# Where a feed-forward product begins in PSUM, and when its turned operand is read back

## The chip, the cores and the metric

One core of one Trainium2 chip runs the whole program. The metric is the device time of one execution in microseconds (us), from launch to end. The profile is one further execution of the same program, recorded by the hardware profiler; its span is counted from the first to the last instruction, and times of single instructions are given from the span's start.

## The reference, cut to what matters

Two transformer layers are computed for 256 tokens of width 2048, in fp32. Each layer has a mixer (sparse and linear attention in the first, stick-breaking attention in the second), then a gated feed-forward part, then a gated projection of a side input. The change lies in the feed-forward part alone, which is run once in each layer with hidden width 5632:

```
def _swiglu(h, norm_g, w_gate, w_up, w_down):
    xn = _rmsnorm(h, norm_g)
    return (jax.nn.silu(xn @ w_gate) * (xn @ w_up)) @ w_down
```

## The kernel before

**Products.** Every fp32 operand is split into a high part and a low rest, and a product is the sum of three matmuls (high by high, high by low, low by high; L235 to L237). Weights arrive in tiles `raw` of 1 MB by SyncE's queue, in three buffers that take turns. ScalarE casts half a tile at a time to `whi` (L106), VectorE subtracts to get `wlo` (L107), and TensorE runs 12 matmuls of 512 columns on the pair. Such a half tile of work is called a half unit here. There are four buffers of `whi` and of `wlo`, so that ScalarE and VectorE run some half units ahead of TensorE.

**Blocks of the feed-forward part** (`ffn`). The 11 column blocks of 512 hidden units stand in groups of three, three, three and two. `gate_up` computes one hidden block: both 128-token halves of gate and of up. The first block is computed plainly (`gate_up_8`); the ten others use a scheme with seven in place of eight products on a part of the rows (`gate_up_7`), with sums of weights that VectorE makes in the tile `work` (L858 to L860), and matmuls at L849. `down` multiplies the hidden blocks of one group by 512 columns of the third weight and adds the result to `h` (L268). While the hidden blocks of one group are computed, the four `down` blocks of the group before are put between them: one after the first hidden block, one after the second, two after the third; the group of two gets two after each. So there are eight places in a layer where a `down` block follows a `gate_up_7` directly, four of them followed by one `down` block and four by two (in layer 0, the last `down` blocks of the program part follow behind the eighth place). The last four `down` blocks come at the end.

**PSUM.** There are eight banks of 128 x 512. `mm_tile` hands out banks 0 to 3 in turn by the counter `turns["mm"]`, and a block takes two. `gate_up_7` does not ask for banks: it writes all eight by number, the gate halves in banks 0 and 1, the up halves in banks 2 and 3. When the gate is complete, VectorE adds a correction to banks 0 and 1, and when the up product is complete, to banks 2 and 3 (both L902, two banks at once). The first matmul into a bank waits until its last reader is done. Since the counter is not touched by `gate_up_7`, the bank with which the next `down` begins depends on how many blocks were handed out before.

**The way of the hidden block.** After the second L902, VectorE multiplies by the silu of the gate (L930, tile `sl`). The block has to be turned, tokens against hidden units, for `down`. `cross` does it with 32 x 32 transposes on VectorE into `tq` (L143), four transfers to DRAM (`ty`, L147) and two back (`tx`, L151), all six issued by GpSimd. `split_hid` then reads `tx` back: ScalarE casts it to `hH` (L920), VectorE subtracts to `hL` (L921).

**What sets the order.** `later` puts a step into a list, and `tick`, called after each half unit, runs the head of the list when it is due; `need` runs it at once. `split_hid` is due so many half units after `cross` ran. This is the order in which the program is written; a scheduler then sets each engine's own order, from what it takes to be ready when. Each engine works through its own list in that order.

Of the kernel before, what the change touches and what calls it, by code (L numbers as in the profile page):

```python
# [27 lines left out]
def trunk_kernel(ctx: ExitStack, tc: tile.TileContext, x, p, even_norm, even_w_in, even_w_gk,  # L28
# [16 lines left out]
    turns = {"mm": 0, "at": 0}  # L45
# [74 lines left out]
    def rstd_of(key):  # L120
        if key not in rstds:
            v = sm.tile([P, NT], F32, name="var")
            nc.vector.tensor_reduce(v, ss[key], axis=AX.X, op=OP.add)
            nc.vector.tensor_scalar(v, v, 1.0 / D, EPS, op0=OP.mult, op1=OP.add)
            r = sm.tile([P, NT], F32, name="rstd")
            nc.gpsimd.tensor_tensor(r, v, mhalf[:, :NT], OP.pow)
            rstds[key] = r
        return rstds[key]
# [56 lines left out]
    def later(fn, key=None, delay=2, after=None):  # L185

        fill.append((key, state["unit"] + delay, after, fn))

    def need(key):
        while key not in done:  # L190
            run_fill()
# [17 lines left out]
    def unit(ps, stat, k0, cols, first, last, nk=KU, kw0=None, step=KU, pre=None, begun=0):  # L209


        kw0 = k0 if kw0 is None else kw0
        raw = raw_tile()
        n = sum(w for _, _, w in cols)
        for j in range(0, nk, step):
            o = 0
            for wt, c0, w in cols:
                nc.sync.dma_start(raw[:, j:min(j + step, nk), o:o + w],
                                  wt[(kw0 + j) * P:(kw0 + min(j + step, nk)) * P, c0:c0 + w]
                                  .rearrange("(k q) n -> q k n", q=P))  # L220
                o += w
        for j in range(0, nk, 2):
            hi = wp.tile([P, 2, NB], F32R, name="whi")
            lo = wp.tile([P, 2, NB], F32R, name="wlo")
            split_sb(raw[:, j:j + 2, :n], hi[:, :, :n], lo[:, :, :n])
            if pre:
                pre(k0 + j + 2)
            for c in range(2):
                k = k0 + j + c
                for tt in range(NT):  # L230
                    sh = stat[0][:, k, tt * P:(tt + 1) * P]
                    sl = stat[1][:, k, tt * P:(tt + 1) * P]
                    st = first and tt >= begun and j + c == 0
                    en = last and j + c == nk - 1
                    nc.tensor.matmul(ps[tt][:, :n], sh, hi[:, c, :n], start=st, stop=False)  # L235
                    nc.tensor.matmul(ps[tt][:, :n], sh, lo[:, c, :n], start=False, stop=False)  # L236
                    nc.tensor.matmul(ps[tt][:, :n], sl, hi[:, c, :n], start=False, stop=en)  # L237
            tick()
# [588 lines left out]
    def ffn(i, xs, nkey, nx_fn, fp):  # L827
        nblk = FF // NB
        groups = [list(range(a, min(a + 3, nblk))) for a in range(0, nblk, 3)]
        hT = {}  # L830
# [20 lines left out]
        def pair(j, b):  # L851

            raw = raw_tile().rearrange("p (r c) n -> p r c n", r=2)
            for c, w in enumerate((ffn_w_gate[i], ffn_w_up[i])):
                nc.sync.dma_start(raw[:, :, c], w[2 * j * P:(2 * j + 2) * P, b * NB:(b + 1) * NB]
                                  .rearrange("(k q) n -> q k n", q=P))

            nc.vector.tensor_tensor(T[:, 0:2], raw[:, 0], raw[:, :, 1], OP.add)  # L858
            nc.vector.tensor_tensor(T[:, 2], T[:, 1], raw[:, 0, 0], OP.add)
            nc.vector.tensor_tensor(T[:, 3], T[:, 2], raw[:, 1, 0], OP.add)  # L860

            def tok(c, t):
                return [x[:, 2 * j + c, t * P:(t + 1) * P] for x in xs]

            def comb(n):
                return [ST[:, hl, n, j] for hl in range(2)]

            pieces = [(raw[:, 0, 0:1], [(B1, tok(0, 0))]), (T[:, 0:2], [(B5, comb(0)), (B7, comb(2))]),
                      (T[:, 2:4], [(B6, comb(1)), (B4, tok(1, 1))]),
                      (raw[:, 1], [(B2, tok(1, 0)), (B3, comb(3))])]  # L870
            for n, (src, ps) in enumerate(pieces):
                hi = wp.tile([P, 2, NB], F32R, name="whi")
                lo = wp.tile([P, 2, NB], F32R, name="wlo")
                split_sb(src, hi[:, :len(ps)], lo[:, :len(ps)])
                for c, (p, stat) in enumerate(ps):
                    product(p, stat, hi[:, c], lo[:, c], j == 0, j == NS - 1 and p >= B1)
                if n % 2:
                    tick()

        def gate_up_7(b):  # L880
            need(("sT", i))
            rest = [(n, k) for n in range(2) for k in range(2 * NS, KC, KU)]

            def classical(n, k):
                nk = min(KU, KC - k)
                unit([bank[:, 2 * n], bank[:, 2 * n + 1]], xs, k, [((ffn_w_gate[i], ffn_w_up[i])[n], b * NB, NB)],
                     n == 1 and k == 2 * NS, k + nk == KC, nk=nk, begun=1)

            for j in range(NS):
                pair(j, b)  # L890
                if j < NS - 1:
                    classical(*rest.pop(0))
            nc.scalar.copy(E[:, 0], bank[:, B1])
            nc.vector.tensor_tensor(E[:, 2], bank[:, B6], E[:, 0], OP.add)
            nc.vector.tensor_tensor(E[:, 1], bank[:, B7], E[:, 2], OP.add)
            nc.vector.tensor_tensor(E[:, 3], bank[:, B5], E[:, 1], OP.subtract)
            nc.vector.tensor_tensor(E[:, 2], bank[:, B5], E[:, 2], OP.subtract)
            for n in range(2):
                while rest and rest[0][0] == n:
                    classical(*rest.pop(0))  # L900
                e = E[:, 2 * n:2 * n + 2]
                nc.vector.tensor_tensor(e, bank[:, 2 * n:2 * n + 2], e, OP.add)  # L902
                if n == 0:
                    sl = fp.tile([P, NT, NB], F32, name="sl", bufs=1)
                    for tt in range(NT):
                        nc.scalar.activation(sl[:, tt], E[:, tt], AF.Silu, scale=rstd_of(nkey)[:, tt:tt + 1])
            return sl, [E[:, 2 + tt] for tt in range(NT)]

        def gate_up_8(b):
            pg = block(xs, [(ffn_w_gate[i], b * NB, NB)], key=nkey)  # L910
            rs = rstd_of(nkey)
            sl = fp.tile([P, NT, NB], F32, name="sl", bufs=1)
            for tt in range(NT):
                nc.scalar.activation(sl[:, tt], pg[tt], AF.Silu, scale=rs[:, tt:tt + 1])
            later(sums_of_operand, key=("sT", i))
            return sl, block(xs, [(ffn_w_up[i], b * NB, NB)])

        def split_hid(dst, x, k0):
            d = [dst[n][:, k0:k0 + 4, :].rearrange("p m (q r) -> p m q r", q=8) for n in range(2)]
            nc.scalar.copy(d[0], x)  # L920
            nc.vector.tensor_tensor(d[1], x, d[0].bitcast(F32), OP.subtract)  # L921

        def gate_up(gi, n):
            b = groups[gi][n]
            if n == 0:
                hT[gi] = (fp.tile([P, 12, NT * P], F32R, name="hH"), fp.tile([P, 12, NT * P], F32R, name="hL"))
            sl, pu = gate_up_7(b) if b else gate_up_8(b)
            rs = rstd_of(nkey)
            for tt in range(NT):
                nc.vector.scalar_tensor_tensor(sl[:, tt], pu[tt], rs[:, tt:tt + 1], sl[:, tt], op0=OP.mult,  # L930
                                               op1=OP.mult)
            x = {}
            later(lambda: x.update(x=cross(sl, fp)), key=("xT", i, b))
            later(lambda: split_hid(hT[gi], x["x"], 4 * n), key=("hT", i, b), after=(("xT", i, b), 10))

        def down(gi, cb, nx):
            for b in groups[gi]:
# [8 lines left out]
        for gi, g in enumerate(groups):  # L946
            for n in range(len(g)):
                gate_up(gi, n)
                if gi:
                    for cb in range(4 * n // len(g), 4 * (n + 1) // len(g)):  # L950
                        down(gi - 1, cb, None)
# [162 lines left out]
```

## Time and profile before

| | |
|---|---|
| median of 3 runs | 2458.12 us (2457.89 to 2463.89) |
| profiled execution, its own time | 2457.39 us |
| span of the profiled execution | 2455.7 us |
| TensorE matmul busy | 2394.8 us, 98% of the span |
| VectorE busy | 1718.6 us, 70% |
| ScalarE busy | 1259.2 us, 51% |
| mean granted TensorE clock | 0.995 of full speed |

Busy time is the sum of an engine's instructions. The feed-forward part of layer 0 lies at about 390 to 1120 us of the span, that of layer 1 at about 1610 to 2345 us. A line "PE bank L235 <- DVE work L902" says that TensorE's matmul of line 235, writing a bank, waited for VectorE's instruction of line 902.

### The profile page before, as it was taken

The page shows a single profiled execution, that of the slowest core. Times are in us where ns is not written, and L with a number is a line of the kernel's source. Part 1 is how long each engine was busy: PE and PEld are TensorE (multiplying, and loading weights), DVE is VectorE, ACT ScalarE, POOL GpSimd, SP SyncE. Part 2 cuts the span into 40 slices and gives each one's busy share as a digit, 9 for nine tenths or more (in the row PEclk, how much of TensorE's full clock was granted, in tenths as well). Part 3 has the DMA queues.
Part 4 walks back from the last instruction along what each step waited for, and adds up shares of the span by engine and source line. Part 5 has one row for each costly group of instructions (what it writes and reads, how often), then busy time and mean ns, then how long its engine had stood idle before and what let it go on. Part 6 is the DMA issues. An engine that isn't in the chain of part 4 may idle for free.

```text
span 2455.7 us, 28118 instructions
## 1 busy us (share of the span) xinstructions
PE 2394.8 (98%) x10786; PEld 1965.8 (80%) x10786; DVE 1718.6 (70%) x2009; ACT 1259.2 (51%) x1560; POOL 105.3 (4%) x177
## 2 busy tenths in 40 slices
PE   8999999999999999999999999999899999999998
PEld 7887788777888888888888888887688888878887
DVE  4765556878877877755666666568778788777565
ACT  6644444545545545446545565545444455444464
POOL 0000000000000000000000000001000000000000
PEclk9999999999999999999999999999999999999999
DMA  6454465566666666555554545656566666666563
GB/s 210 149 164 154 147 213 189 182 204 206 207 230 206 206 223 222 192 194 180 173 188 162 170 165 172 206 171 209 178 208 218 216 206 214 214 223 204 180 233 121
DMA packets 240681, 473.13 MB, mean 193 GB/s; under 512 B 12849, under 2 KB 19729, under 8 KB 240418
## 3 DMA queue, kind: packets, MB, share of 16 engines
q1 hardware_dynamic: 232514, 447.07, 54.7%
q0 software_dynamic: 7744, 23.08, 2.9%
q8 instruction: 84, 1.38, 0.2%
q10 hardware_dynamic: 288, 1.18, 0.1%
q14 instruction: 51, 0.42, 0.1%
HBM read 457.66 MB, written 13.63 MB: 192 GB/s over the span
## 4 chain that ended last, share of the span: by engine, by line
PE 80%; DVE 8%; DMA 7%; ACT 3%; issue 2%; POOL 0%; SPq 0%; DVEq 0%; POOLq 0%; ACTq 0%
PE bank L235 23%; PE bank L236 23%; PE bank L237 23%; PE bank L849 8%; DVE wlo L107 3%; DMA raw<-in_ffn_w_up_dram 3%; DMA tx<-ty 1%; DMA raw<-in_odd_w_in_dram 1%; DMA ty<-tq 1%; DVE work L902 1%; PE bank L165 1%; DVE kT L135 1%; ACT whi L106 1%; DVE sl L930 1%; DVE tq L143 0%
## 5 line engine op out<-in xcount | busy, mean ns | idle before, releaser
L107 DVE TENSOR_TENSOR wlo<-raw,whi 128x1024 fp32r<-128x1024 f32 (+2 forms) x848 | 982.3, 1172 | 481.6 <-ACT whi L106 477.6
L106 ACT CAST whi<-raw 128x1024 fp32r<-128x1024 f32 (+2 forms) x848 | 843.1, 1011 | 852.7 <-PE bank L237 583.7
L235 PE MATMUL bank<-whi,aH 128*128 128x512 f32 (+2 forms) x2176 | 850.2, 391 | 1.1 <-ACT whi L106 1.1
L236 PE MATMUL bank<-wlo,aH 128*128 128x512 f32 (+2 forms) x2176 | 843.1, 388 | 4.8 <-DVE wlo L107 4.5
L237 PE MATMUL bank<-whi,aL 128*128 128x512 f32 (+2 forms) x2176 | 842.2, 387 | 0.0
L236 PEld LDWEIGHTS bank<-wlo,aH 128*128 128x128 f32 x2176 | 409.7, 188 | 89.0 <-DVE wlo L107 8.8
L235 PEld LDWEIGHTS bank<-whi,aH 128*128 128x128 f32 x2176 | 409.6, 188 | 85.3 <-issue 2.8
L237 PEld LDWEIGHTS bank<-whi,aL 128*128 128x128 f32 x2176 | 409.1, 188 | 84.6 <-issue 1.0
L235 PE MATMUL bank<-whi,hH 128*128 128x512 f32 x704 | 276.6, 393 | 16.9 <-DVE work L902 16.9
L236 PE MATMUL bank<-wlo,hH 128*128 128x512 f32 x704 | 276.2, 392 | 0.0
L237 PE MATMUL bank<-whi,hL 128*128 128x512 f32 x704 | 276.1, 392 | 0.0
L106 ACT CAST whi<-work 128x1024 fp32r<-128x1024 f32 x120 | 126.4, 1053 | 188.8 <-PE bank L237 126.3
L107 DVE TENSOR_TENSOR wlo<-work,whi 128x1024 fp32r<-128x1024 f32 x120 | 146.6, 1221 | 65.8 <-ACT whi L106 65.4
L849 PE MATMUL bank<-whi,sT 128*128 128x512 f32 x480 | 171.1, 396 | 11.7 <-ACT whi L106 11.7
L235 PEld LDWEIGHTS bank<-whi,hH 128*128 128x128 f32 x704 | 132.2, 188 | 50.3 <-ACT whi L106 19.8
L236 PEld LDWEIGHTS bank<-wlo,hH 128*128 128x128 f32 x704 | 132.3, 188 | 28.4
L237 PEld LDWEIGHTS bank<-whi,hL 128*128 128x128 f32 x704 | 132.3, 188 | 28.0
L849 PEld LDWEIGHTS bank<-whi,sT 128*128 128x128 f32 x480 | 91.6, 191 | 32.4 <-ACT whi L106 13.4
L849 PE MATMUL bank<-wlo,sT 128*128 128x512 f32 x240 | 95.1, 396 | 3.2 <-DVE wlo L107 3.2
L858 DVE TENSOR_TENSOR work<-raw 128x1024 f32<-128x1024 f32 x60 | 73.3, 1222 | 34.6 <-DMA raw<-in_ffn_w_up_dram 34.2
L147 POOL DMA_DIRECT2D ty<-tq x88 | 48.5, 561 | 1140.8 <-DVE tq L143 988.7
L849 PE MATMUL bank<-wlo,aH 128*128 128x512 f32 x180 | 72.7, 404 | 7.0 <-DVE wlo L107 7.0
(253 smaller groups left out, 1624.7 us busy)
## 6 DMA issues: line engine op xcount, KB each, us to landing
raw<-in_ffn_w_down_dram SPq DMA_DIRECT2D x88, 1024.0 KB, 5.7
raw<-in_ffn_w_gate_dram SPq DMA_DIRECT2D x48, 1024.0 KB, 5.2
raw<-in_ffn_w_up_dram SPq DMA_DIRECT2D x48, 1024.0 KB, 5.2
raw<-in_odd_w_in_dram SPq DMA_DIRECT2D x48, 1024.0 KB, 5.1
raw<-in_ffn_w_gate_dram SPq DMA_DIRECT2D x80, 512.0 KB, 3.9
raw<-in_ffn_w_up_dram SPq DMA_DIRECT2D x80, 512.0 KB, 5.3
raw<-in_even_w_in_dram SPq DMA_DIRECT2D x36, 1024.0 KB, 5.0
raw<-in_ple_w_gate_dram SPq DMA_DIRECT2D x28, 1024.0 KB, 5.1
```

What stands on the lines that cost most here:

```text
L106: nc.scalar.copy(hi, raw)
L107: nc.vector.tensor_tensor(lo, raw, hi.bitcast(F32), OP.subtract)
L135: nc.vector.transpose(dst[32 * a:32 * a + 32, :, :, 32 * q:32 * q + 32], src.rearrange("p t (m a c) -> p t m a c", a=4, c=32)[32 * q:32 * ...
L147: nc.gpsimd.dma_start(y[:, :, q].rearrange("a c t n -> c a (t n)"), tq[32 * q:32 * q + 32].rearrange("c a t m r -> c a (t m r)"))
L165: nc.tensor.transpose(ps[:, c, tt, :], h[:, tt, k * P:(k + 1) * P], ident)
L235: nc.tensor.matmul(ps[tt][:, :n], sh, hi[:, c, :n], start=st, stop=False)
L236: nc.tensor.matmul(ps[tt][:, :n], sh, lo[:, c, :n], start=False, stop=False)
L237: nc.tensor.matmul(ps[tt][:, :n], sl, hi[:, c, :n], start=False, stop=en)
L849: nc.tensor.matmul(bank[:, p], a, b, start=first and m == 0, stop=last and m == 2)
L858: nc.vector.tensor_tensor(T[:, 0:2], raw[:, 0], raw[:, :, 1], OP.add)
L902: nc.vector.tensor_tensor(e, bank[:, 2 * n:2 * n + 2], e, OP.add)
L930: nc.vector.scalar_tensor_tensor(sl[:, tt], pu[tt], rs[:, tt:tt + 1], sl[:, tt], op0=OP.mult, op1=OP.mult)
```

## The change

Two lines. At the end of `gate_up_7` the counter of banks is set to 0, so that the block behind it begins with banks 0 and 1. And `split_hid` becomes due 16 half units after its `cross` ran, not 10.

```diff
--- before.py
+++ after.py
@@ -904,6 +904,7 @@
                     sl = fp.tile([P, NT, NB], F32, name="sl", bufs=1)
                     for tt in range(NT):
                         nc.scalar.activation(sl[:, tt], E[:, tt], AF.Silu, scale=rstd_of(nkey)[:, tt:tt + 1])
+            turns["mm"] = 0
             return sl, [E[:, 2 + tt] for tt in range(NT)]
 
         def gate_up_8(b):
@@ -931,7 +932,7 @@
                                                op1=OP.mult)
             x = {}
             later(lambda: x.update(x=cross(sl, fp)), key=("xT", i, b))
-            later(lambda: split_hid(hT[gi], x["x"], 4 * n), key=("hT", i, b), after=(("xT", i, b), 10))
+            later(lambda: split_hid(hT[gi], x["x"], 4 * n), key=("hT", i, b), after=(("xT", i, b), 16))
 
         def down(gi, cb, nx):
             for b in groups[gi]:
```

TensorE's order at the first `down` block of layer 0, with the engines whose semaphores a row waits for; the rows above are the end of `gate_up_7`. First before, then with the change:

```order
L237 MATMUL bank<-whi,aL 128x512
L235 MATMUL bank<-whi,hH 128x512 [waits DVE_49,Activation_49,Pool_49]
L236 MATMUL bank<-wlo,hH 128x512
L237 MATMUL bank<-whi,hL 128x512
L235 MATMUL bank<-whi,hH 128x512
```

```order
L237 MATMUL bank<-whi,aL 128x512
L235 MATMUL bank<-whi,hH 128x512 [waits Activation_49,Pool_49]
L236 MATMUL bank<-wlo,hH 128x512 [waits DVE_49]
L237 MATMUL bank<-whi,hL 128x512
L235 MATMUL bank<-whi,hH 128x512
```

The first matmul of the block no longer waits for VectorE; the second one waits for it instead, for its own `wlo`. Before, 12 first matmuls of `down` blocks have the wait for VectorE (six in each layer), with the change none has. No matmul is added or removed.

VectorE's order after the hidden block that ends group 0 (third block of each layer): the transpose `tq` behind the products with the silu. First before, then with the change, where lines behind 906 are numbered one higher:

```order
L902 TENSOR_TENSOR work<-bank,work 128x1024
L107 TENSOR_TENSOR wlo<-raw_3966,whi 128x1024
L930 SCALAR_TENSOR_TENSOR sl<-work,rstd,sl 128x512 x2
L107 TENSOR_TENSOR wlo<-raw,whi 128x1024
L143 STREAM_TRANSPOSE tq<-sl 128x8x4x32
L107 TENSOR_TENSOR wlo<-raw,whi 128x1024
L859 TENSOR_TENSOR work<-work,raw 128x512
```

```order
L902 TENSOR_TENSOR work<-bank,work 128x1024
L107 TENSOR_TENSOR wlo<-raw_3964,whi 128x1024
L931 SCALAR_TENSOR_TENSOR sl<-work,rstd,sl 128x512 x2
L107 TENSOR_TENSOR wlo<-raw,whi 128x1024 x2
L143 STREAM_TRANSPOSE tq<-sl 128x8x4x32
L859 TENSOR_TENSOR work<-work,raw 128x512
```

The transpose stands one `wlo` later. The read-back of the same block, further down in VectorE's list:

```order
L107 TENSOR_TENSOR wlo<-work,whi 128x1024
L860 TENSOR_TENSOR work<-work,raw 128x512
L921 TENSOR_TENSOR hL<-tx,hH 128x1024
L107 TENSOR_TENSOR wlo<-work,whi 128x1024
L107 TENSOR_TENSOR wlo<-raw,whi 128x1024 x2
L894 TENSOR_TENSOR work<-bank,work 128x512
```

```order
L107 TENSOR_TENSOR wlo<-work,whi 128x1024
L860 TENSOR_TENSOR work<-work,raw 128x512
L107 TENSOR_TENSOR wlo<-work,whi 128x1024
L922 TENSOR_TENSOR hL<-tx,hH 128x1024
L107 TENSOR_TENSOR wlo<-raw,whi 128x1024
L894 TENSOR_TENSOR work<-bank,work 128x512
```

The read-back `hL` stands one `wlo` later, and in ScalarE's list `hH` stands one `whi` later at the same place. The read-back of the block before it (second block of each layer) stands where it stood. Of the 22 read-backs of the program, 12 keep their place and 10 move by one cast on ScalarE and by one to two rows on VectorE.

## Rows read from the trace of the kernel before

**Rows 1.** The page: span and instructions.

```profile
span 2455.7 us, 28118 instructions
```

**Rows 2.** Waits, whole span, TensorE's and ScalarE's: us in total, times, longest.

```profile
PE bank L235 <- DVE work L902: 16.9, 12, 1.4
PE bank L849 <- ACT whi L106: 11.7, 4, 3.7
PE bank L849 <- DVE wlo L107: 10.2, 12, 2.5
...
ACT hH L920 <- DMA tx<-ty: 24.5, 5, 6.7
```

**Rows 3.** Timeline of TensorE: start, us, line, tiles, idle before and its releaser.

```profile
575.18 0.47 PE L235 MATMUL bank<-whi,hH 128*128 128x512 f32 x1 [1.41 <-DVE work L902]
...
591.75 0.40 PE L849 MATMUL bank<-whi,aH 128*128 128x512 f32 x1
...
633.02 0.39 PE L237 MATMUL bank<-whi,aL 128*128 128x512 f32 x1
633.25 0.39 PE L235 MATMUL bank<-whi,hH 128*128 128x512 f32 x1
```

**Rows 4.** The chain of work that ended last: start, us, what; L902 pieces.

```profile
573.81 1.24 DVE work L902
...
633.45 1.23 DVE work L902
...
692.28 1.24 DVE work L902
...
768.40 1.23 DVE work L902
...
828.02 1.23 DVE work L902
...
886.82 1.24 DVE work L902
...
1858.03 1.22 DVE work L902
...
1917.59 1.23 DVE work L902
...
2053.31 1.23 DVE work L902
...
2112.15 1.24 DVE work L902
```

**Rows 5.** Timeline of VectorE behind the hidden block that ends at 573.6 us.

```profile
573.81 1.23 DVE L902 TENSOR_TENSOR work<-bank,work 128x1024 f32<-128x1024 f32 x1 [0.41 <-PE bank L237]
...
579.71 1.18 DVE L107 TENSOR_TENSOR wlo<-raw,whi 128x1024 fp32r<-128x1024 f32 x1
```

**Rows 6.** Timeline of TensorE, pair at 664 us.

```profile
664.29 0.50 PE L849 MATMUL bank<-wlo,aH 128*128 128x512 f32 x1 [0.22 <-DVE wlo L107]
```

**Rows 7.** Timeline of ScalarE at layer 1's second read-back.

```profile
1774.15 1.04 ACT L920 CAST hH<-tx 128x1024 fp32r<-128x1024 f32 x1 [6.34 <-DMA tx<-ty]
1775.10 1.04 ACT L106 CAST whi<-work 128x1024 fp32r<-128x1024 f32 x1
```

**Rows 8.** Timeline of TensorE at the second read-backs, layer 0 and layer 1.

```profile
553.22 0.50 PE L849 MATMUL bank<-whi,sT 128*128 128x512 f32 x1 [1.65 <-ACT whi L106]
554.67 0.50 PE L849 MATMUL bank<-wlo,sT 128*128 128x512 f32 x1 [0.95 <-DVE wlo L107]
...
1776.19 0.50 PE L849 MATMUL bank<-whi,sT 128*128 128x512 f32 x1 [3.34 <-ACT whi L106]
1777.64 0.50 PE L849 MATMUL bank<-wlo,sT 128*128 128x512 f32 x1 [0.95 <-DVE wlo L107]
```

**Rows 9.** Windows: stretch, us, busy (x) of PE, PEld, DVE, ACT, POOL, granted clock, DMA.

```profile
1778.00:1781.00 3.00, 3.00 (x9) 2.31 (x8) 3.00 (x4) 2.50 (x3) 0.00 (x0) 0.52 0.30 63
552.00:554.00 2.00, 0.50 (x1) 0.19 (x1) 1.75 (x2) 2.00 (x3) 0.00 (x0) 1.00 0.00 0
```

## The prediction, made before the changed kernel ran

> **What bounds the kernel now.** I read the page first: the span is 2455.7 us [rows 1], and TensorE's matmuls are busy for 98% of it, so only what TensorE waits for can be won. The waits come next, grouped over the whole span [rows 2]. The largest item of TensorE is the one that the first line of the change speaks of: 12 times a matmul waits for VectorE's L902, 16.9 us in all, 1.41 us each time. Behind it come 11.7 and 10.2 us of waits at L849 for `whi` and `wlo`. ScalarE's list holds the reason for part of these: its read-back cast `hH` waits 24.5 us in five instances for `tx` to land, and what stands behind it in its queue waits as well.
>
> The timeline shows the wait for L902 in place [rows 3]. At 575.18 us the first matmul of a `down` block starts after 1.41 us of idle time, since the counter gave it bank 2, which L902 is reading [rows 5]. At 633.25 us another `down` block starts 0.23 us after the last matmul of its `gate_up_7`, with no gap: there the counter stood at bank 0, and L902 reads banks 2 and 3. So the kernel already contains what the change wants everywhere: of the eight places of a layer the counter is right at two and wrong at six. The chain of work tells what this is worth. It passes through an L902 at each of the eight places. At the six it goes on to the waiting matmul; at the two (633.45 and 828.02 in layer 0 [rows 4]) TensorE does not wait for it, and the chain goes on through VectorE and a load of weights and comes back to TensorE only later.
>
> **First line: the bank.** Nothing is computed differently; 12 first matmuls lose a wait. The lists of instructions show just this: the wait for VectorE moves from the block's first matmul to its second, which waits for its own `wlo`. What takes the place of the wait? Three things could.
>
> The first is `wlo`. VectorE does L902, one `wlo`, the two products with silu, a sum and the transpose in one run, and the next `wlo` ends at 579.71 + 1.18 = 580.89 us [rows 5]. With four buffers this is the fifth half unit of the block. A block of six half units takes 591.75 - 575.18 = 16.57 us [rows 3], 2.76 each, so the fifth starts at 575.18 + 4 x 2.76 = 586.2 us now and at 584.8 without the wait. That leaves 3.9 us to spare. The Trainium skill (PSUM — Partial Sum Buffer, section "Engine vs sequencer instructions") says that the queues of ScalarE, VectorE and GpSimd are strictly first in, first out, while matmuls start in order. By that rule alone a wait that TensorE loses at L902 could come back at the next operand behind L902, and the gain would be 0 in place of 1.41; the row with 3.9 us to spare speaks against it here.
>
> The second is the bank itself. Banks 0 and 1 were last read by the first L902 of the same hidden block, before the whole up product, so they are free. After one `down` block, though, the next `gate_up_7` writes bank 1 with its thirteenth matmul, about 12 x 0.23 = 2.8 us behind the end of `down`, and VectorE must have added bank 1 to `h` by then. The cycles without a wait have this layout today, so their length includes it.
>
> The third is the loads of weights, and here there are twins to read. A cycle is the time from one L902 to the next, with one `down` and one `gate_up_7` between. With the wait it takes 633.45 - 573.81 = 59.64 us, or 828.02 - 768.40 = 59.62 [rows 4]. Without it, the four such cycles of the program take 58.83, 58.80, 59.56 and 58.84 us (692.28 - 633.45, 886.82 - 828.02, 1917.59 - 1858.03, 2112.15 - 2053.31), 59.01 in the mean. So of 1.41 us a place with one `down` keeps 59.63 - 59.01 = 0.62, between 0.07 and 0.84. The rest is lost where the pair of L849 catches up with its operand: 0.22 us show as a wait at 664.29 us [rows 6]. There are four such places in the program: 4 x 0.62 = 2.5 us, bounds 4 x 0.07 = 0.3 and 4 x 1.41 = 5.6.
>
> The other eight places have two or more `down` blocks behind them and no twin without the wait. In a second `down` VectorE has 16.57 us more in which to catch up, and the chain there goes from L902 through TensorE to the next L902, so I take the full wait: 8 x 1.41 = 11.3 us. The lower bound is that they lose as much as the others, 8 x 0.62 = 5.0.
>
> **Second line: the read-back.** It does much less than it says. The scheduler puts an instruction where it takes it to be ready, and of 22 read-backs 12 do not move and the others move by one or two rows. The first bad read-back of each layer, that of the second block, is among the 12, so its stall stays whole. The other is that of the third block, where `hH` waits 6.34 us in layer 1 [rows 7]. There TensorE waits 3.34 us for a `whi` that stands behind `hH`, then 0.95 for its `wlo` [rows 8]; in layer 0 it waits 1.65 and 0.95. With the change that `whi` stands ahead of `hH`, so six matmuls run before the stall; but the transpose stands one `wlo` later, which shifts the round trip by 1.18 us [rows 5]. In layer 1, `hH` would start at 1774.15 + 1.18 = 1775.33. The next cast starts 0.95 later, the first matmul on it 1.09 after that and the second another 1.45 (steps of [rows 7, 8]): 1778.82 us. Today the same matmul, at full clock, comes six matmuls behind 1777.64: 1779.02. So 0.2 us are won, in each layer: 0.4. Bounds: if the stall vanishes, 1.65 + 0.95 + 3.34 + 0.95 = 6.9 us, and 1.4 for the clock (below), 8.3; if the later round trip costs its 1.18 us twice and the clock falls in layer 0 too, a loss of 3.8.
>
> The clock is the open point here. After the idle 3.34 us in layer 1 the granted clock is 0.52 from 1778 to 1781 us, the lower of the two levels, 1.2 GHz of 2.4; in layer 0, around the idle 1.65 us, it is 1.00 [rows 9]. Three microseconds at 0.52 cost 3.00 x 0.48 = 1.4 us. The stall in layer 1 stays about as long (it starts six matmuls later and ends 1.2 us later), so I let the clock fall there as now. The Trainium skill (TensorE: Matmul & The Clock Gate, section "HAM oscillation — how this bites in real kernels") says that idle gaps throw TensorE back to its lower clock and that each costs a start at that level. By it a shorter gap in layer 1 would bring 1.4 us more, a longer one in layer 0 would cost 1.4; the rows show both sides, and the sum takes neither.
>
> **The sum** against the profiled execution: 11.3 + 2.5 + 0.4 = 14.2 us, so 2457.39 - 14.2 = 2443.2 us. The median of the runs shown is 0.73 us above the profiled time, within their own spread, so I predict 2443. About 0.3%, 7.4 us, is what a measurement of this kernel can tell from no change.
>
> **The rivals.**
>
> More comes back: the 12 waits go whole (16.9 us), and the second read-back stall shrinks to half with the clock kept (about 4): 2457.4 - 20.9 = 2436.5. For it: in the first group the transpose of the next block moves ahead of a sum, which gets its transfers out of the way of the loads. Against it: the twins.
>
> The loads take more: the places with two `down` blocks keep 0.62 us too, since the raw tiles come in the same rotation there: 12 x 0.62 = 7.4 us, 2450.0. For it: the four twins lose between 0.6 and 1.3 us of their 1.41. Against it: no wait at L849 is on the chain in the long cycles.
>
> Nothing is won: the wait comes back at the next `wlo`, 2457. It needs VectorE to be 3.9 us later than in [rows 5].
>
> The read-back loses its stalls altogether, also the first in each layer: the 24.5 us of ScalarE's wait go, and with them at most the 11.7 + 10.2 = 21.9 us of L849 waits [rows 2]: 2443.2 - 21.9 = 2421. It needs `hH` to move past the landing of `tx`; one cast is no such move.
>
> Slower: the later transpose lets `ty` and `tx` of the third block run into the next loads of weights, and TensorE idles longer at that one read-back in each layer. It decides only from a loss above 13.8 us in two places, 7 each, where the longest wait of `hH` in the program is 6.7 [rows 2]. With 8 each it would be 2457.4 - 13.8 + 16 = 2460; against it, the round trip has moved by one instruction.
>
> **How the numbers follow.** Forecast as summed: 0.62. More comes back: 0.13. The loads take more: 0.14, about half of it on either side of the 0.3% line at 2450.7. Nothing: 0.06. Stalls gone: 0.02. Slower: 0.03. Faster by over 0.3%: 0.62 + 0.13 + 0.02 + 0.08 = 0.85; same 0.06 + 0.06 = 0.12; slower 0.03. The range reaches to the two neighbours of the forecast, 2436 to 2451, and leaves out the last three cases and the tails.
>
> **What would show it.** The line "PE bank L235 <- DVE work L902" should be gone from TensorE's waits. Cycles with one `down` should take about 59.0 us, those with two about 74.7 where one now takes 768.40 - 692.28 = 76.12 [rows 4]. ScalarE's wait of `hH` for `tx` should stay above 20 us, with the first stall of each layer as now. The prediction is wrong if the L849 waits grow by more than 4 us, if a matmul of `down` waits for `wlo`, or if the granted clock falls at a place where it is 1.00 now.

## The result, and the profile after

The change takes 2436.55 us (median of four runs, 2435.57 to 2438.25) against 2461.01 us before (2457.89 to 2464.57) in the same comparison: ratio 0.9901, 95% interval 0.9889 to 0.9914. The profiled execution takes 2435.57 us, 21.8 us less than the profiled one of before. So it is faster, 6.5 us below the forecast, and inside the range by 0.6 us. As a gain it is 24.4 us by the ratio and 21.8 by the profiles, where 14.2 were forecast, and most of the surplus has one place.

The page and the waits of the changed kernel (us in total, times, longest), which answer to [rows 1, 2]:

```profile
span 2433.9 us, 28109 instructions
...
PE bank L849 <- DVE wlo L107: 12.3, 17, 3.0
PE bank L849 <- ACT whi L106: 5.5, 2, 3.1
...
ACT hH L921 <- DMA tx<-ty: 14.4, 4, 6.1
```

The wait of L235 for L902 is gone. That much was forecast. Not forecast is the second line: four waits of L849 for `whi` have become two, and `hH` has 14.4 us of waiting left of 24.5. To see where, I take the program apart by the second L902 of each hidden block, as in the prediction. VectorE's timeline of the change, from the third hidden block's L902 on (start, us, line, tiles; the last two rows are layer 1):

```profile
526.42 1.22 DVE L902 TENSOR_TENSOR work<-bank,work 128x1024 f32<-128x1024 f32 x1
...
568.40 1.22 DVE L902 TENSOR_TENSOR work<-bank,work 128x1024 f32<-128x1024 f32 x1
...
626.36 1.23 DVE L902 TENSOR_TENSOR work<-bank,work 128x1024 f32<-128x1024 f32 x1 [0.20 <-PE bank L237]
...
685.38 1.23 DVE L902 TENSOR_TENSOR work<-bank,work 128x1024 f32<-128x1024 f32 x1 [0.41 <-PE bank L237]
...
759.86 1.22 DVE L902 TENSOR_TENSOR work<-bank,work 128x1024 f32<-128x1024 f32 x1
...
1741.66 1.22 DVE L902 TENSOR_TENSOR work<-bank,work 128x1024 f32<-128x1024 f32 x1
...
1783.24 1.22 DVE L902 TENSOR_TENSOR work<-bank,work 128x1024 f32<-128x1024 f32 x1 [0.41 <-PE bank L237]
```

The same view of before for the third block, where [rows 4] begin one block later (the last two rows are layer 1's third and fourth block):

```profile
529.40 1.22 DVE L902 TENSOR_TENSOR work<-bank,work 128x1024 f32<-128x1024 f32 x1
...
1750.70 1.22 DVE L902 TENSOR_TENSOR work<-bank,work 128x1024 f32<-128x1024 f32 x1
...
1798.39 1.23 DVE L902 TENSOR_TENSOR work<-bank,work 128x1024 f32<-128x1024 f32 x1 [0.41 <-PE bank L237]
```

The cycle with two `down` blocks, 685.38 to 759.86, takes 74.48 us, where it took 76.12. The one before it, with one `down`, takes 59.02; the prediction said 74.7 and 59.0. But from the third block's L902 to the fourth's (called the third block's stretch below), with no `down` in between and hence no wait for L902 in either kernel, it is 568.40 - 526.42 = 41.98 us against 573.81 - 529.40 = 44.41, and in layer 1 41.58 against 47.69. These two stretches alone bring 8.5 us. All of the span's 21.8 us, from such differences: cycles with two `down` blocks 8.6 (six, 1.44 each), with one 0.6 (eight), the third block's read-back 8.5, the second block's 0.7, the stretch ahead of the first L902 2.2 (the change touches nothing there, and over the kernels below this start lies between 478.1 and 481.3 us), between the layers -0.4, and the end 1.6. The 2.2 and the -0.4 hold a matter of the clock: behind the first pair of layer 0 it is 0.57 for four microseconds before and 1.00 with the change, behind that of layer 1 it is the other way round, and 4 x 0.43 = 1.7 us each is what that is worth.

Not all of the 14.4 us is left over. At the last hidden block of layer 0 the wait of `hH` is new:

```profile
1049.56 1.05 ACT L921 CAST hH<-tx 128x1024 fp32r<-128x1024 f32 x1 [2.56 <-DMA tx<-ty]
```

There the next load of weights goes out 1.2 us behind the start of `ty`'s issue, where it went out 2.9 us behind, and the way through DRAM takes 8.0 us, where it took 5.1. TensorE does not wait there. The first line alone does the same and the second alone does not, so it is the counter that moved this load.

What happened at the third block is seen on four engines. The change, timelines of VectorE, SyncE, GpSimd and ScalarE (start, us, line, tiles, idle before), then windows of the same place in both layers (granted clock third from the end):

```profile
530.01 2.35 DVE L107 TENSOR_TENSOR wlo<-raw,whi 128x1024 fp32r<-128x1024 f32 x2
...
532.39 0.37 SPq L855 DMA_DIRECT2D raw<-in_ffn_w_gate_dram  x1
532.81 0.46 SPq L855 DMA_DIRECT2D raw<-in_ffn_w_up_dram  x1
...
533.81 2.20 POOL L147 DMA_DIRECT2D ty<-tq  x4 [39.20 <-DVE tq L143]
...
539.75 1.50 POOL L151 DMA_DIRECT2D tx<-ty  x2 [3.73 <-ACT whi L106]
...
546.50 1.04 ACT L921 CAST hH<-tx 128x1024 fp32r<-128x1024 f32 x1
...
547.00:550.00 3.00, 3.00 (x15) 2.31 (x13) 3.00 (x3) 3.00 (x5) 0.00 (x0) 1.00 0.05 18
...
1761.00:1765.00 4.00, 4.00 (x19) 3.34 (x18) 3.13 (x3) 4.00 (x5) 0.00 (x0) 1.00 0.21 78
```

Before, VectorE, GpSimd, SyncE and ScalarE:

```profile
535.29 1.18 DVE L107 TENSOR_TENSOR wlo<-raw,whi 128x1024 fp32r<-128x1024 f32 x1
...
535.66 2.19 POOL L147 DMA_DIRECT2D ty<-tq  x4 [38.97 <-DVE tq L143]
...
536.50 0.37 SPq L855 DMA_DIRECT2D raw<-in_ffn_w_gate_dram  x1
536.92 0.49 SPq L855 DMA_DIRECT2D raw<-in_ffn_w_up_dram  x1
...
543.93 1.50 POOL L151 DMA_DIRECT2D tx<-ty  x2 [6.07 <-ACT whi L106]
...
551.17 1.05 ACT L920 CAST hH<-tx 128x1024 fp32r<-128x1024 f32 x1 [4.65 <-DMA tx<-ty]
```

`hH` no longer waits, TensorE has no gap and the clock stays at 1.00, where before it fell to 0.52 in layer 1 [rows 9]. (The read-backs that [rows 7, 8] call second ones are this third block's.) The way through DRAM, from the issue of `ty` to the issue of `tx`, takes 539.75 - 533.81 = 5.94 us; before it took 543.93 - 535.66 = 8.27. What differs around it is a load of weights: 1 MB in two halves by SyncE's queue. Before, it goes out 0.8 and 1.3 us behind the issue of `ty`; now 1.4 and 1.0 us ahead of it. The `wlo` past which the transpose was moved is the last reader of a `raw` tile, and when it ends, SyncE may load into that tile: before, it ends at 535.29 + 1.18 = 536.47 us and the load goes out at 536.50; now the two `wlo` end at 530.01 + 2.35 = 532.36, and it goes out at 532.39. With the `wlo` ahead of the transpose, the load passes the `ty` transfers.

### The profile page after: what moved, and what is told of

It is laid out like the page before. It is cut to its first block, busy times and chain, and to the rows that moved or that the text cites. A ratio compares the mean times of both kernels' runs of the same rounds, so it can differ in the third digit from the quotient of the medians.

```text
span 2433.9 us, 28109 instructions
## 1 busy us (share of the span) xinstructions
PE 2393.8 (98%) x10786; PEld 1965.1 (81%) x10786; DVE 1716.8 (71%) x2009; ACT 1258.4 (52%) x1560; POOL 105.6 (4%) x177
## 3 DMA queue, kind: packets, MB, share of 16 engines
q10 hardware_dynamic: 288, 1.18, 0.1%
## 4 chain that ended last, share of the span: by engine, by line
PE 71%; DVE 11%; DMA 10%; ACT 3%; issue 3%; SPq 0%; POOL 0%; DVEq 0%; POOLq 0%; ACTq 0%
PE bank L236 20%; PE bank L235 20%; PE bank L237 20%; PE bank L849 6%; DMA raw<-in_ffn_w_up_dram 6%; DVE wlo L107 6%; DMA raw<-in_odd_w_in_dram 2%; ACT whi L106 1%; DVE kT L135 1%; PE bank L165 1%; DVE work L858 1%; DMA raw<-in_ffn_w_down_dram 1%; DMA tx<-ty 1%; DVE sl L931 1%; DVE work L902 1%
## 5 line engine op out<-in xcount | busy, mean ns | idle before, releaser
L235 PE MATMUL bank<-whi,aH 128*128 128x512 f32 (+2 forms) x2176 | 849.7, 391 | 0.7 <-ACT whi L106 0.7
L235 PEld LDWEIGHTS bank<-whi,aH 128*128 128x128 f32 x2176 | 409.8, 188 | 84.9 <-issue 2.8
L235 PE MATMUL bank<-whi,hH 128*128 128x512 f32 x704 | 277.2, 394 | 0.0
L849 PE MATMUL bank<-whi,sT 128*128 128x512 f32 x480 | 170.2, 394 | 5.5 <-ACT whi L106 5.5
L235 PEld LDWEIGHTS bank<-whi,hH 128*128 128x128 f32 x704 | 132.2, 188 | 30.0
L849 PEld LDWEIGHTS bank<-whi,sT 128*128 128x128 f32 x480 | 91.2, 190 | 25.3 <-ACT whi L106 6.3
L849 PE MATMUL bank<-wlo,sT 128*128 128x512 f32 x240 | 94.8, 395 | 1.9 <-DVE wlo L107 1.9
L849 PE MATMUL bank<-wlo,aH 128*128 128x512 f32 x180 | 73.3, 407 | 10.8 <-DVE wlo L107 10.4
```

Source lines behind the costliest of these rows:

```text
L849: nc.tensor.matmul(bank[:, p], a, b, start=first and m == 0, stop=last and m == 2)
```

## The experiments

All runs are compared with before on their own chip, and their ratios are to it. Edits are shown against the changed kernel, cut at "...". The theory of the first experiments: the order of that load and of `ty` makes the surplus. Its rival: the read-back, which also stands one cast later, makes it.

**One line of the change at a time.** The first line alone (due again after 10 half units), and the second line alone (no `turns["mm"] = 0`):

```diff
-            later(lambda: split_hid(hT[gi], x["x"], 4 * n), key=("hT", i, b), after=(("xT", i, b), 16))
+            later(lambda: split_hid(hT[gi], x["x"], 4 * n), key=("hT", i, b), after=(("xT", i, b), 10))
```

> The first line of the change alone (the counter set to 0, the read-back due after 10 half units as before). If the two lines simply add, this kernel has lost the 12 waits for L902 but has the stall at the third block's read-back in both layers as before (TensorE waits there near 1.65 and 3.3 us plus 0.95 each). By the cycles of the changed kernel that stall cost 2.4 us in layer 0 and 6.1 in layer 1, so this kernel should be 8.5 us slower than the changed one: about 2445 us, some 13 us faster than before. By the step of the prediction that gave the second line only 0.4 us it should stand at the changed kernel's time, 2436 to 2437 us.

Measured: 2448.94 us, ratio 0.9952 (0.9936 to 0.9969), 11.8 us below before by the ratio. `hH` waits as before at the third block, 5.96 us in layer 0 and 5.62 in layer 1; `ty` to `tx` takes 8.4 and 8.3 us.

```diff
-            turns["mm"] = 0
```

> The kernel before with the second line of the change alone; the counter of banks stays as it was, so the 12 waits for L902 are there (about 16.9 us of idle time on TensorE, 12 instances). Transfers theory (the late transpose puts the next 1 MB load ahead of the ty transfers): the third block's transpose stands one wlo later here too, so its read-back waits for nothing, its cycle is 41.5 to 42.5 us as in the change, and the time is 7 to 10 us below before. Additive rival by the first theory of the prediction (the read-back brings 0.4 us): within 2 us of before. If the shorter wait for L902 is needed for the effect (the load's place against ty depends on it), hH still waits above 2 us at the third block and the gain is below 5 us.

Measured: 2451.28 us, ratio 0.9962 (0.9950 to 0.9975), 9.4 us below before. The waits for L902 are there (17.3 us, 12), and the third block's stretch takes 41.97 and 42.83 us, where the whole change has 41.98 and 41.58. The two lines add up within their intervals: 11.8 + 9.4 = 21.2, with 24.4 for both. The second line is worth about as much as the first, where the prediction gave it 0.4.

**Transpose or read-back.** The second line moves two things at the third block. Four combinations with the first line in place: the run with the first line alone has neither. This one makes the transpose of the third block due 4 half units after the products with silu, not 2, and the read-back goes along behind it:

```diff
+            later(lambda: x.update(x=cross(sl, fp)), key=("xT", i, b), delay=4 if b == 2 else 2)
...
+            later(lambda: split_hid(hT[gi], x["x"], 4 * n), key=("hT", i, b), after=(("xT", i, b), 10))
```

> The first line, the read-back due after 10 half units, and the third block's turning made due two half units later. The orders of the engines at the third block are then those of the changed kernel (transpose one wlo later, read-back one cast later), and only read-backs of later blocks stand one row elsewhere. Both theories of the read-back expect the stall at the third block to be gone and 2436 us, within 2 us of the changed kernel. If something else in the 16 half units matters, it is slower by up to 8 us.

Measured: 2435.95 us, ratio 0.9904 (0.9880 to 0.9928), the time of the change; no wait of `hH` there, `ty` to `tx` 5.95 and 5.79 us. Now the read-back late and the transpose where it stood (its casts queued behind a certain `whi` and `wlo`):

```diff
...
+            later(lambda: split_hid(hT[gi], x["x"], 4 * n, mark[3, 2, 2] if b == 2 else None), key=("hT", i, b),
+                  after=(("xT", i, b), 10))
```

> As the kernel before in this call (the third block's turning two half units later in the changed kernel's order), but with the third block's transpose put back ahead of the wlo, and the read-back held where it is. Theory 1 (what counts is that this wlo frees its raw tile and so sends the next 1 MB of weights off ahead of the transfers ty, not among them): the weights are issued about 1 us behind ty again, tx lands some 2 us later, the stall is back, less the 1.4 us of matmuls that now run ahead of it: 2442 to 2445 us, with hH waiting for tx 5 to 6 us in each layer at the third block. Theory 2 (what counts is that the read-back stands one cast later): no stall at the third block, 2436 us.

Measured: 2445.11 us, ratio 0.9932 (0.9909 to 0.9956); `ty` to `tx` 8.42 and 8.47 us, `hH` waits 2.36 and 1.90, less than the 5 to 6 us that the theory named. And the transpose late, the read-back put back ahead of the last cast of `work`:

```diff
...
+                if (b, j, n) == (3, 2, 2):
+                    need(("hT", i, 2))
+                    with tc.issue_after(back[0].ins):
+                        nc.scalar.copy(hi, src)
...
```

> The counterpart: the third block's transpose stays behind the wlo as in the changed kernel, and the read-back is put ahead of the last cast of work again, where it stood before. Theory 1 (the order of load and transfer): the round trip stays short, hH waits for tx less than 1 us at the third block, and the time is 2436 to 2438 us. Theory 2 (the place of the read-back): the stall is back as before, 2444 to 2446 us, with waits of TensorE near 1.65 and 3.3 us at L849 for whi.

Measured: 2438.09 us, ratio 0.9909 (0.9889 to 0.9930); `ty` to `tx` 5.67 and 7.56 us, `hH` waits 1.06 and 4.48, where the theory named less than 1. These runs are of one chip, so the medians can be set against each other: the late transpose brings 2448.94 - 2438.09 = 10.9 and 2445.11 - 2435.95 = 9.2 us, the late read-back 3.8 and 2.1, which the scatter of these runs (2437.84 to 2447.44 in the third of the four) could make by itself. The transpose it is, for the most part. That it acts through the load is not shown by that: several things move with it.

**The load alone.** The next kernel is the changed one with the instructions of every engine in the same order. Only the load at the third block gets one dependency more, on the sum behind the transpose:

```diff
...
+                if (j, b) == (2, 3):
+                    tc.add_manual_dep(ld.ins, hold[0].ins.name, mybir.DependencyInfo(
+                        mybir.DependencyClass.Sync, mybir.DependencyReason.DATA), reason="hold")
...
+            hold[:] = [nc.vector.tensor_tensor(T[:, 2], T[:, 1], raw[:, 0, 0], OP.add)]
```

> The changed kernel with one more dependency and every engine's instructions in the same order: at the third hidden block of each layer the 1 MB load that SyncE sends 1.4 and 1.0 us before the first ty transfer must wait for the sum L859 behind the transpose, and so goes out about 0.4 and 0.8 us behind ty's issue. Transfers theory: ty to tx takes 8 to 8.7 us instead of 5.7 to 5.9, hH waits 2 to 4 us at this block again, the cycle of that block takes 44 to 46 us instead of 41.5 to 42, and the time is 4 to 8 us above that of the change, 2440 to 2444. Rival (the transpose's own place counts, the load is a bystander): ty to tx stays below 6 us, hH does not wait, and the time is within 2 us of the change.

Measured: 2448.53 us, ratio 0.9945 (0.9932 to 0.9958), 12.0 us above the change by the medians, 10.8 by the ratios. That is the transfers theory, with more than the 4 to 8 us it named. Its trace, timelines of GpSimd, SyncE, ScalarE and TensorE, a window, and the landing time of the load's second half (median us from issue):

```profile
537.80 2.20 POOL L147 DMA_DIRECT2D ty<-tq  x4 [39.84 <-DVE tq L143]
...
545.86 1.50 POOL L151 DMA_DIRECT2D tx<-ty  x2 [5.86 <-DMA ty<-tq]
...
538.14 0.37 SPq L855 DMA_DIRECT2D raw<-in_ffn_w_gate_dram  x1
538.56 0.46 SPq L855 DMA_DIRECT2D raw<-in_ffn_w_up_dram  x1
...
554.94 1.04 ACT L924 CAST hH<-tx 128x1024 fp32r<-128x1024 f32 x1 [4.36 <-DMA tx<-ty]
...
556.98 0.80 PE L849 MATMUL bank<-whi,aH 128*128 128x512 f32 x1 [3.02 <-ACT whi L106]
558.43 0.80 PE L849 MATMUL bank<-wlo,aH 128*128 128x512 f32 x1 [0.65 <-DVE wlo L107]
...
557.00:560.00 3.00, 2.35 (x5) 1.55 (x6) 3.00 (x4) 3.00 (x4) 0.00 (x0) 0.50 0.20 15
560.00:563.00 3.00, 3.00 (x9) 2.33 (x8) 3.00 (x5) 0.25 (x1) 0.00 (x0) 0.50 0.92 349
...
raw<-in_ffn_w_up_dram SPq DMA_DIRECT2D x1, 512.0 KB, 5.9
```

The two halves of the load go out 0.3 and 0.8 us behind `ty`, and `tx` is issued 8.06 us after `ty` (8.78 in layer 1). `hH` waits 4.36 us, then TensorE 3.02 and 0.65, and the clock lies at 0.50 from 557 to 563 us, which costs another 6 x 0.50 = 3.0 us. Together that is 6.7 us. The third block's stretches take 48.60 and 46.65 us, 6.6 and 5.1 more than in the change, 11.7 together, so these two places hold the whole loss. A later load could also cost by itself, so in another run it waits for a `wlo` still further down:

```diff
...
+                lo_op = split_sb(src, hi[:, :len(ps)], lo[:, :len(ps)])
+                hold[:] = [lo_op] if n == 1 else hold
```

> As the run before it, but the load waits for a wlo further behind the transpose, and goes out about 2.5 to 3 us behind ty's issue. Transfers theory: it meets the round trip later, ty to tx takes 5.5 to 7 us as at the other places with a load 2 to 3.3 us behind ty, hH waits less than 1.5 us, and the time is 0 to 3 us above that of the change, below that of the run before it. Rival (a load that is sent later costs time because its own weights land later): this run loses more than the run before it, 6 us or more above the change.

Measured: 2435.89 us, ratio 0.9897 (0.9882 to 0.9913), the time of the change, and 12.6 us below the run before it on the same chip. The same rows of this run:

```profile
534.62 2.20 POOL L147 DMA_DIRECT2D ty<-tq  x4 [37.66 <-DVE tq L143]
...
539.96 1.50 POOL L151 DMA_DIRECT2D tx<-ty  x2 [3.15 <-ACT whi L106]
...
537.26 0.37 SPq L855 DMA_DIRECT2D raw<-in_ffn_w_gate_dram  x1
537.68 0.50 SPq L855 DMA_DIRECT2D raw<-in_ffn_w_up_dram  x1
...
546.99 1.04 ACT L925 CAST hH<-tx 128x1024 fp32r<-128x1024 f32 x1
...
raw<-in_ffn_w_up_dram SPq DMA_DIRECT2D x1, 512.0 KB, 5.5
```

2.3 us later still, the load costs nothing: `ty` to `tx` takes 5.34 us, `hH` does not wait. (The scheduler also moved some of VectorE's `wlo` and sums behind the transpose by a few rows here; in the run before it no row of any engine moved.) So at this block the load costs time when it goes out 0.3 or 0.8 us into the 2.20 us in which GpSimd issues the four `ty` transfers; 1.4 us ahead of their start or 2.6 us behind it, it does not. With this the cause of the surplus is shown: it is the order of one load and four transfers. Why the transfers take longer in one order than in the other is not shown.

**The same at the second block.** The stall of the second block, 5.35 and 6.13 us of waiting of `hH`, is the same collision, if the theory holds. Its rows in the change:

```profile
484.37 2.20 POOL L147 DMA_DIRECT2D ty<-tq  x4 [36.59 <-DVE tq L143]
...
493.11 1.50 POOL L151 DMA_DIRECT2D tx<-ty  x2 [6.54 <-DMA ty<-tq]
...
485.20 0.37 SPq L855 DMA_DIRECT2D raw<-in_ffn_w_gate_dram  x1
485.62 0.50 SPq L855 DMA_DIRECT2D raw<-in_ffn_w_up_dram  x1
...
500.57 1.04 ACT L921 CAST hH<-tx 128x1024 fp32r<-128x1024 f32 x1 [5.35 <-DMA tx<-ty]
```

So the transposes of the second and third block are made due two half units later (4 for 2), and in another run three (5 for 2). The read-back goes along, so this does not part the two as the runs above did for the third block:

```diff
-            later(lambda: x.update(x=cross(sl, fp)), key=("xT", i, b))
+            later(lambda: x.update(x=cross(sl, fp)), key=("xT", i, b), delay=4 if 0 < b < 3 else 2)
```

> The changed kernel with the transposes of the second and third hidden block due 4 half units after silu's products instead of 2. The second block's transpose then stands one wlo later, as the third's does in the change. Transfers theory: its ty to tx takes 5 to 6.5 us instead of 8 to 8.7, hH at the second block waits less than 2 us instead of 5.4 and 6.1, and the cycle from the second block's L902 on gets 5 to 7 us shorter in each layer: 10 to 15 us below the change, about 2423. Rival (the length of the transfers hangs on the region of the span, not on the order of load and transfers): ty to tx stays above 8 us, hH waits 4 to 5 us, and the time is within 3 us of the change.

> The changed kernel with the same two transposes due 5 half units after silu's products, so that they stand behind a wlo of the sums too, and the read-backs behind the next L902. If only the distance of the read-back from the landing matters, hH waits nowhere in these blocks and the time is as in the run with 4 half units, or 1 to 3 us better. If the later read-back holds up the first down block that needs it, TensorE waits for hT there, and the time is 2 to 8 us above that run.

Measured: 2425.49 us, ratio 0.9860 (0.9846 to 0.9874), and 2424.44 us, ratio 0.9855 (0.9842 to 0.9869). Both beat the change by 10 to 12 us and before by some 35; between the two there is no difference that can be told. The second block in the first of them:

```profile
487.00 0.37 SPq L855 DMA_DIRECT2D raw<-in_ffn_w_gate_dram  x1
487.42 0.46 SPq L855 DMA_DIRECT2D raw<-in_ffn_w_up_dram  x1
...
488.43 2.20 POOL L147 DMA_DIRECT2D ty<-tq  x4 [40.39 <-DVE tq L143]
...
494.50 1.50 POOL L151 DMA_DIRECT2D tx<-ty  x2 [3.88 <-ACT whi L106]
...
501.78 1.05 ACT L921 CAST hH<-tx 128x1024 fp32r<-128x1024 f32 x1 [0.62 <-DMA tx<-ty]
```

The load goes ahead, `ty` to `tx` takes 6.07 us instead of 8.74, the wait shrinks from 5.35 to 0.62, and the stretch from the second block's L902 to the third's takes 42.05 and 41.54 us instead of 48.32 and 49.07.

**The four places with one `down`.** The profiles of before and after alone show 0.6 us of gain there, not 2.5, as if the loads ate it all. To test this, the wait was put back in these four places:

```diff
-            turns["mm"] = 0
+            turns["mm"] = 2 if b in (3, 6) else 0
```

> The changed kernel with the counter at 2 instead of 0 at the two places of a layer that have one down block ahead and begin a new group (blocks 3 and 6), so that the wait for L902 is back in four places, 1.41 us each. Loads theory (what these places win is lost again in the same or the next cycle, which waits for loads of weights): the time is that of the change, within 1.5 us, though 5.6 us of idle time at L902 return. Twins of the prediction (0.62 each): 2.5 us slower than the change. Rival (each wait is worth its length): 5.6 us slower.

Measured: 2439.00 us, ratio 0.9916 (0.9903 to 0.9930), 3.7 us above the change by the ratios. The interval of this difference is about 4.5 us to either side, so it holds all three expectations; the run does not decide. The traces taken together say more. The eight cycles with one `down` add up to 474.6 and 477.3 us in the two profiles with all the waits for L902 (before, and the second line alone; four of the eight cycles contain one), 478.5 in this run, and 472.0 to 474.3, 473.2 in the mean, in the nine profiles without it. That is a gain of about 2.7 us (475.9 - 473.2), so the 0.6 of the two single profiles can be scatter, and that the loads eat all of it is unlikely. The figure is rough: the two profiles with all the waits differ by 2.7 themselves.

## Why the prediction was right, and where it was wrong

- **What bounds, and the first line: right.** The wait for L902 is gone, nothing of its kind came back at the `wlo` behind it: no such wait stands behind a `down` block's first matmul. The rule on strict queues of the Trainium skill (PSUM — Partial Sum Buffer, section "Engine vs sequencer instructions") would have allowed it; the 3.9 us to spare, read from [rows 5], spoke against it.
- **The long places: right in size.** Forecast 1.41 us each; the six whose cycle can be read bring 8.62 / 6 = 1.44. The rival that had the loads take half of it does not fit that.
- **The places with one `down`: about right.** 2.5 us forecast from the twins, about 2.7 over the profiles, 0.6 in the one pair of before and after; the run made to test it did not decide.
- **The second line: wrong.** The step that failed is "the transpose stands one `wlo` later, which shifts the round trip by 1.18 us". It took the length of the round trip as given and moved it. But the transpose passed the `wlo` that frees a `raw` tile, so a load changed places with `ty`, and the round trip got 8.27 - 5.94 = 2.3 us shorter. The term of 0.4 us measured 8.5 in the profiles and 9.4 as a run of its own; the upper bound of 8.3, the stall gone with its cost in clock, is what came. Two of its rivals speak of transfers and loads, but no sentence of the prediction looked up where SyncE's loads go out against `ty`.
- **The range held by luck.** The measured time lies 0.6 us above its lower end, and what brought it there is a term that was priced at 0.4 us and came twenty times as large.
- **The rivals.** "More comes back" has almost the measured number, 2436.5, but by another sum: the 12 waits did not come back whole (8.6 us in six places and about 2.7 in four, where 10 times 1.41 is 14.1), and the read-back did not halve its stalls but lost them at one block. Its remark on transfers that get "out of the way of the loads" names the mechanism, but for the next block, where `ty` to `tx` takes 5.03 us before and 4.86 after and `hH` waits in neither. The "slower" rival named the right mechanism, `ty` and `tx` meeting the loads, with the wrong sign: they met already before. That a stall goes only if `hH` moves past the landing of `tx` was wrong too: a shorter way brings the landing forward.
- **What was to show it.** Cycles of 59.0 and 74.7 came as 59.24 (mean of eight) and 74.77 (mean of six). `hH` was to wait above 20 us in all and waits 14.4: this line was the one that told that a step had failed. The L849 waits did not grow. The clock did fall at one place where it was 1.00, behind the first pair of layer 1; the change does not reach there, and in layer 0 the same place went the other way, so this sign told nothing:

```profile
450.00:454.00 4.00, 3.98 (x11) 3.14 (x12) 4.00 (x6) 1.67 (x2) 0.00 (x0) 0.57 0.63 152
1673.00:1677.00 4.00, 4.00 (x18) 3.31 (x19) 4.00 (x6) 2.00 (x2) 0.00 (x0) 1.00 0.64 156
```

```profile
1663.00:1667.00 4.00, 4.00 (x13) 3.10 (x12) 4.00 (x6) 1.99 (x2) 0.00 (x0) 0.57 0.78 219
```

The first two rows are windows of before, the last is one of the change (granted clock third from the end); in the change the place in layer 0 has 1.00.

One thing stays open: with the second line alone, layer 1's third block has the load 1.4 us ahead of `ty` and still takes 7.28 us to `tx`, with 1.35 us of waiting; its layer 0 takes 5.74 with the same order. And in the run with the transpose late and the read-back early, layer 1 takes 7.56 us. Something besides the order of this load moves the length by up to 2 us, and the places below with a load 2.0 us behind scatter as much.

## What to carry to other kernels

When an instruction is moved past another on one engine, ask what the other one releases: here a reader of a buffer in rotation, and so a 1 MB load on another queue. A transfer that everything waits for (a turn through DRAM above all) has no fixed length; read beside it which loads go out from shortly before its issue to its landing, and try to put them ahead of it or clearly behind. And a small effect per place is read from many profiles, not from one pair.

## What the runs showed of the hardware

The time from `ty` to `tx` depends on where the nearest load of weights stands. Read from the timelines of SyncE and GpSimd of all twelve kernels, at all 22 hidden blocks of each:

| the next load goes out, against the start of `ty`'s issue | places | `ty` to `tx`, us |
|---|---|---|
| 1.4 us ahead (and none until 5 us behind) | 12 | 5.67 to 6.19, but twice 7.28 and 7.56 |
| 0.3 us behind | 2 | 8.06, 8.78 |
| 0.8 us behind | 27 | 8.10 to 8.91 |
| 1.2 us behind (last block of layer 0) | 9 | 7.91 to 8.09 |
| 1.5 or 1.6 us behind (first blocks, with another 1.8 or 1.9 us ahead) | 24 | 7.60 to 9.65 |
| 2.0 us behind | 78 | 5.85 to 8.15, more than half of them up to 6.2 |
| 2.2 to 2.6 us behind | 72 | 5.21 to 6.83, all but one up to 6.2 |
| 2.9 to 3.3 us behind | 22 | 4.80 to 5.34 |
| 4.2 to 5.8 us behind | 18 | 4.90 to 6.14 |

The way that was taken for a fixed length goes from about 5 to about 8.5 us as the load comes 2.4 us nearer to the start of the issue, and falls again when the load goes out ahead of it. It is the `ty` transfers that take longer: at the third block of layer 0 the slowest of the four lands 6.1 us after its issue before, 4.2 in the change, 6.2 with the load held and 3.3 with the load held more. At the third block of layer 0 before, the load's second half lands 6.5 us after its issue at 536.92, at 543.4 us, and `tx` is issued 0.5 us later; with the load held it lands at 538.56 + 5.9 = 544.5, and `tx` comes 1.4 us later; with the load held more, `tx` is issued at 539.96, 3.2 us before the load's second half lands at 543.2. The line of before from which the first of these comes:

```profile
raw<-in_ffn_w_up_dram SPq DMA_DIRECT2D x1, 512.0 KB, 6.5
```

So a load that is sent between the `ty` transfers lands near the end of their way or ahead of it, and one that is sent 2.6 us behind their start lands well after it. The Trainium skill (DMA: Bandwidth & Descriptors, section "Queues, rings and completion order") says that the increment which reports a transfer lands only after every earlier write of the same DMA engine, across its queues. The three cases are compatible with that, but no run here took the transfers' completion and their data apart.

The length of one gap does not settle the clock here. After 3.02 and 0.65 us of idle time in the run with the load held it lies at 0.50, the lower level, for six microseconds, while before, 1.65 and 0.95 us with matmuls between left it at 1.00 [rows 8, 9]. But before also has a single gap of 2.39 us, at 450 us, with 0.57 behind it, and one of 2.46 us, at 1673 us, with 1.00 behind it.
